# A decoder kernel's first loads: the first row and its norm parameters on ScalarE's queue

## The chip, the cores and the metric

The kernel runs on one core of a Trainium2 chip. The metric is the device time of one execution in microseconds. A core has five engines with a program each: TensorE (PE, with its weight loads as PEld), VectorE (DVE), ScalarE (ACT), GpSimd (POOL) and SyncE (SP). SP computes nothing; it issues transfers (DMAs). ScalarE and GpSimd can issue transfers too. An engine takes its instructions in order and waits at each until what it needs is there.

## The reference

Two layers on a residual x of 512 tokens by 1024: differential softmax attention, then retention, each followed by a squared-ReLU MLP and a gated embedding. Only the first step matters here: a norm, and the projection to queries, keys and values.

```
def rms_norm(x, g):
    y = x * rsqrt(mean(x * x, axis=-1) + EPS)
    return y * g
...
h = rms_norm(x, norm_mix[0])
qkv = h @ a_w_qkv          # values first in this kernel: 1024 x 1024
...
lam = exp(sum(lam_q1 * lam_k1)) - exp(sum(lam_q2 * lam_k2)) + lambda_init
```

## The kernel before

The residual lies transposed: eight rows of tiles xT[k], each 128 features by 512 tokens in float32 (256 KB). Precision is kept by splitting every factor into a high part (fp32r) and a low part, and multiplying three times: high by high (L188), high by low and low by high (L189, L190).

The weights come in tiles of 128x1024 (512 KB) by SP's queue into raw; ScalarE casts raw to wh (L84) and VectorE subtracts for wl (L88). There are three raw buffers and five of wh and wl. `W.load()` issues a tile; for the first tile W.parts is 2, and it comes in two halves of 256 KB.

The beginning works so. `sm` holds all small parameters, 128x311 floats: columns 0 to 15 are the gains of the mixers' norms (C_MIX), 16 to 31 those of the MLPs' norms (C_MLP on), then those of the embeddings' norms and the attention's gains, and at the end 256 columns of the lambda vectors. It is SP's first load. Then a loop over k = 0 to 7 loads row xin k of x, makes its scaled halves (`make_z`: zh = x times gain on ScalarE, L168; zl on VectorE, L169), loads a weight tile at each even k, and adds the squares of x (`squares`: ScalarE L234 for the first row and L237 for the others, GpSimd L238 adds them into acc_a). The norm's factor itself is applied behind the matmul, so that the projection doesn't wait for it.

TensorE first runs nine warm-up matmuls on a tile of ones (L288). Then the value projection goes over k, four accumulators (pv) a step: 12 matmuls for each k, two k to a weight tile, so raw0 serves k = 0 (first half) and k = 1 (second half), raw1 serves k = 2 and 3, raw2 k = 4 and 5.

The lambda factor (lp, ls, nlam) and the attention's gains (gq, gs) are written behind the projection in the source, at L341 to L355. The scheduler puts instructions of one engine in an order of its own, by when their inputs should be there; only loads marked keep_in_program_order stay in the order of the source.

Of the kernel before, what the change touches and what calls it, by code (L numbers as in the profile page):

```python
# [10 lines left out]
F32 = mybir.dt.float32  # L11
# [5 lines left out]
P = 128  # L17
# [3 lines left out]
KD = D // P  # L21
# [12 lines left out]
C_MIX, C_MLP, C_PE = 0, 16, 32  # L34
# [67 lines left out]
def decoder_trunk(ctx: ExitStack, tc, xT, pT, small, dist, decay, ident,  # L102
                  w_v, w_qk, w_o, w_up0, w1_0, w2_0, w_g0,
                  w_rv, w_rqk, w_rg, w_ro, w_up1, w1_1, w2_1, w_g1, out):
    nc = tc.nc

    gp = ctx.enter_context(tc.tile_pool(name="gp", bufs=1))
# [17 lines left out]
    def load(out, in_):  # L125
        tc.keep_in_program_order(nc.sync.dma_start(out=out, in_=in_))

    def slot(name, dt=F32):
        return gp.tile([P, T], dt, name=name, tag="slot", bufs=SLOTS)
# [96 lines left out]
    def make_z(src, gain_col, k, make=slot):  # L226
        zh = make(f"zh{gain_col}_{k}", F32R)
        zl = make(f"zl{gain_col}_{k}", F32R)
        split_into(zh, zl, src, sm[:, gain_col + k : gain_col + k + 1])
        return zh, zl  # L230

    def squares(acc, src, k, engine=None):
        if k == 0:
            tc.keep_in_program_order(nc.scalar.activation(out=acc, in_=src, func=AF.Square))  # L234
        else:
            sq = slot("sq")
            nc.scalar.activation(out=sq, in_=src, func=AF.Square)  # L237
            (engine or nc.gpsimd).tensor_tensor(out=acc, in0=acc, in1=sq, op=ALU.add)  # L238
# [33 lines left out]


    sm = gp.tile([P, N_SMALL], F32, name="sm")
    load(sm, small)
    eps = gp.tile([P, 1], F32, name="eps")
    nc.vector.memset(eps, EPS)
    ones = gp.tile([P, P], F32, name="ones")
    nc.vector.memset(ones, 1.0)
    ones_r = gp.tile([P, P], F32R, name="ones_r")  # L280
    nc.scalar.copy(out=ones_r, in_=ones)
    mhalf = gp.tile([P, 8], F32, name="mhalf")
# [8 lines left out]
    z = []  # L291
    W.parts = 2
    for k in range(KD):
        t = slot(f"xin{k}")
        load(t, xT[k])
        z.append(make_z(t, C_MIX, k))
        if k % 2 == 0:
            W.load()
            W.parts = 1
        squares(acc, t, k)  # L300
# [384 lines left out]
    with tc.tile_pool(name="zp", bufs=1) as zp:  # L685

        def zslot(name, dt):
            return zp.tile([P, T], dt, name=name, tag="z", bufs=16)
# [12 lines left out]
        with tc.tile_pool(name="ret", bufs=1) as ap:  # L701
# [36 lines left out]
            for h in range(RH):  # L738
# [22 lines left out]
                for n in range(4):  # L761
# [4 lines left out]
                    t = ap.tile([P, T], F32, name="rt", tag="rt", bufs=4)  # L766
# [21 lines left out]
                for jt in range(NT):  # L788
# [7 lines left out]
                    t = ap.tile([P, T], F32, name="rt", tag="rt", bufs=4)  # L796
# [40 lines left out]
            for m in range(KD):  # L837
                pu = (ps_tr if m % 2 == 0 else ps_s)(f"pu1{m}")
                up_unit(pu, wu, p1, m)
                t = zslot(f"pus{m}", F32)  # L840
# [90 lines left out]
```

## Time and profile before

| | us |
|---|---|
| median of 3 runs (1478.69 to 1480.45) | 1480.25 |
| the profiled execution | 1480.16 |
| its span, first to last instruction | 1478.0 |
| TensorE busy | 1468.3 (99%) |
| VectorE, ScalarE, GpSimd busy | 787.4, 650.6, 157.9 |
| chain that ended last: TensorE, ScalarE, VectorE | 94%, 3%, 2% |

The chain that ended last is followed back from the last instruction, at each step to what released it. A row of the timeline gives start, length, engine, line, operation, output and inputs, and in brackets the idle time before it with what ended it. Rows of loads give the size of one and the time from its issue to its landing.

### The profile page before, as it was taken

What the parts mean: (1) busy time and instruction counts of PE and PEld (TensorE: products, weight loads), DVE (VectorE), ACT (ScalarE), POOL (GpSimd) and SP (SyncE); (2) the same over time, 40 slices, a digit from 0 to 9 for tenths busy, and PEclk for the clock granted to TensorE, in tenths of its full rate; (3) what the DMA queues carried; (4) which work ended last, traced back from release to release, by engine and by line L of the source; (5) the groups of instructions that cost most, each with busy time, mean ns of one, the idle gap of its engine ahead of it and who ended that gap; (6) DMA issues with size and microseconds to landing.
All of it is one profiled execution on the core that took longest, in us unless ns stands there. A gap on an engine that the chain in (4) does not pass through costs nothing.

```text
span 1478.0 us, 17131 instructions
## 1 busy us (share of the span) xinstructions
PE 1468.3 (99%) x6668; PEld 1199.8 (81%) x6668; DVE 787.4 (53%) x1189; ACT 650.6 (44%) x1007; POOL 157.9 (11%) x127
## 2 busy tenths in 40 slices
PE   9999999999999999999999999999999999999998
PEld 7777677888888888888888888888878888888887
DVE  6775776643434434485464555553684343434445
ACT  6777777841423224354442532433553231323432
POOL 4112113100000000321120200301220000000020
PEclk9999999999999999999999999999999999999999
DMA  6654466853333332143223232132233233333212
GB/s 227 143 115 114 115 171 145 212 171 99 91 95 100 100 98 90 62 164 124 75 86 110 65 104 93 57 129 71 80 106 99 90 97 100 100 96 92 97 57 86
DMA packets 46880, 159.92 MB, mean 108 GB/s; under 512 B 5200, under 2 KB 5712, under 8 KB 46800
## 3 DMA queue, kind: packets, MB, share of 16 engines
q1 hardware_dynamic: 41328, 138.92, 29.3%
q0 software_dynamic: 4896, 17.83, 6.7%
q10 hardware_dynamic: 576, 2.10, 0.4%
q8 instruction: 52, 0.85, 0.2%
q14 instruction: 28, 0.23, 0.0%
HBM read 136.80 MB, written 4.19 MB: 95 GB/s over the span
## 4 chain that ended last, share of the span: by engine, by line
PE 94%; ACT 3%; DVE 2%; issue 1%; POOL 0%; DMA 0%; SPq 0%; POOLq 0%; ACTq 0%; DVEq 0%
PE py L190 8%; PE py L188 8%; PE py L189 8%; PE ph L188 8%; PE ph L190 8%; PE ph L189 8%; PE rg L188 2%; PE rg L189 2%; PE pg L188 2%; PE pg L189 2%; PE pg L190 2%; PE rv L188 2%; PE rv L190 2%; PE rqk L190 2%; PE rqk L188 2%; PE rv L189 2%
## 5 line engine op out<-in xcount | busy, mean ns | idle before, releaser
L84 ACT CAST wh<-raw 128x1024 fp32r<-128x1024 f32 (+1 forms) x211 | 221.0, 1049 | 603.0 <-PE py L189 235.7
L88 DVE TENSOR_TENSOR wl<-raw,wh 128x1024 fp32r<-128x1024 f32 (+1 forms) x211 | 267.2, 1267 | 54.6 <-ACT wh L84 53.3
L189 PE MATMUL ph<-zl,wh 128*128 128x512 f32 x512 | 199.4, 389 | 0.1
L188 PE MATMUL ph<-zh,wh 128*128 128x512 f32 x512 | 199.2, 389 | 0.0
L190 PE MATMUL ph<-zh,wl 128*128 128x512 f32 x512 | 199.2, 389 | 0.0
L188 PE MATMUL py<-hh,wh 128*128 128x512 f32 x512 | 199.2, 389 | 0.0
L189 PE MATMUL py<-hl,wh 128*128 128x512 f32 x512 | 199.2, 389 | 0.0
L190 PE MATMUL py<-hh,wl 128*128 128x512 f32 x512 | 199.2, 389 | 0.0
L628 DVE TENSOR_TENSOR x<-x,py 128x512 f32<-128x512 f32 x64 | 44.0, 688 | 200.0 <-PE py L190 200.0
L618 DVE SCALAR_TENSOR_TENSOR ht<-ph,rsm 128x512 f32<-128x512 f32 x64 | 44.1, 691 | 158.4 <-PE ph L190 158.2
L189 PEld LDWEIGHTS ph<-zl,wh 128*128 128x128 f32 x512 | 96.1, 188 | 20.9 <-DVE zl L169 0.9
L189 PEld LDWEIGHTS py<-hl,wh 128*128 128x128 f32 x512 | 96.1, 188 | 20.1
L190 PEld LDWEIGHTS py<-hh,wl 128*128 128x128 f32 x512 | 96.1, 188 | 20.0
L190 PEld LDWEIGHTS ph<-zh,wl 128*128 128x128 f32 x512 | 96.1, 188 | 20.0
L188 PEld LDWEIGHTS ph<-zh,wh 128*128 128x128 f32 x512 | 96.1, 188 | 19.9
L188 PEld LDWEIGHTS py<-hh,wh 128*128 128x128 f32 x512 | 96.1, 188 | 19.8
L238 POOL TENSOR_TENSOR acc_p<-acc_p,sq 128x512 f32<-128x512 f32 x14 | 24.5, 1751 | 649.2 <-ACT sq L237 649.2
L188 PE MATMUL pqk<-wh,zh 128*128 128x512 f32 x128 | 52.9, 413 | 0.0
L190 PE MATMUL pqk<-wh,zl 128*128 128x512 f32 x128 | 51.5, 402 | 0.0
L189 PE MATMUL pqk<-wl,zh 128*128 128x512 f32 x128 | 51.4, 401 | 0.0
L188 PE MATMUL pg<-zh,wh 128*128 128x512 f32 (+1 forms) x136 | 51.2, 377 | 0.0
L190 PE MATMUL pg<-zh,wl 128*128 128x512 f32 (+1 forms) x136 | 51.2, 377 | 0.0
(870 smaller groups left out, 2798.3 us busy)
## 6 DMA issues: line engine op xcount, KB each, us to landing
raw<-in_w SPq DMA_DIRECT2D x128, 512.0 KB, 3.6
wl<-raw POOLq DMA_DIRECT2D x34, 512.0 KB, 5.4
raw<-in_w_qk SPq DMA_DIRECT2D x16, 512.0 KB, 4.0
raw<-in_w_g SPq DMA_DIRECT2D x16, 512.0 KB, 3.5
raw<-in_w_rv SPq DMA_DIRECT2D x16, 512.0 KB, 3.6
raw<-in_w_rqk SPq DMA_DIRECT2D x16, 512.0 KB, 4.1
raw<-in_w_rg SPq DMA_DIRECT2D x16, 512.0 KB, 3.5
raw<-in_w_ro SPq DMA_DIRECT2D x16, 512.0 KB, 3.6
```

What stands on the lines that cost most here:

```text
L84: nc.scalar.copy(out=hi[:, s], in_=raw[:, s])
L88: e.tensor_tensor(out=lo[:, r], in0=raw[:, r], in1=hi[:, r].bitcast(F32), op=ALU.subtract)
L188: nc.tensor.matmul(ps, a[0], b[0], start=start, stop=False)
L189: nc.tensor.matmul(ps, a[0], b[1], start=False, stop=False)
L190: nc.tensor.matmul(ps, a[1], b[0], start=False, stop=stop)
L238: (engine or nc.gpsimd).tensor_tensor(out=acc, in0=acc, in1=sq, op=ALU.add)
L618: nc.vector.scalar_tensor_tensor(out=t, in0=s[1], scalar=0.0, in1=rs, op0=ALU.max, op1=ALU.mult)
L628: nc.vector.tensor_tensor(out=x[m], in0=x[m], in1=ps, op=ALU.add)
```

## The change

The load of sm is cut in two. Columns 0 to 15 (the mixers' gains, 64 bytes in a partition) and the first row xin0 are issued by ScalarE, as its first two instructions. The other 295 columns of sm are issued by SP behind xin1. SP's queue so begins with the two halves of the first weight tile. The tiles of all rows xin are claimed ahead of the loop, and the tile of ones is filled before eps.

```
-    load(sm, small)
+
+    def beside(out, in_):
+
+        tc.keep_in_program_order(nc.scalar.dma_start(out=out, in_=in_))
+
+
+    beside(sm[:, 0:C_MLP], small[:, 0:C_MLP])
+    xin = [slot(f"xin{k}") for k in range(KD)]
+    beside(xin[0], xT[0])
+    ones = gp.tile([P, P], F32, name="ones")
+    nc.vector.memset(ones, 1.0)
     eps = gp.tile([P, 1], F32, name="eps")
     nc.vector.memset(eps, EPS)
-    ones = gp.tile([P, P], F32, name="ones")
-    nc.vector.memset(ones, 1.0)
...
     for k in range(KD):
-        t = slot(f"xin{k}")
-        load(t, xT[k])
+        t = xin[k]
+        if k > 0:
+            load(t, xT[k])
+        if k == 1:
+            load(sm[:, C_MLP:], small[:, C_MLP:])
         z.append(make_z(t, C_MIX, k))
```

SP's queue at the start of the program, before. In all these rows the name's first number is the tile's (raw0, xin1), what follows an underscore is a buffer's number, and the brackets name the semaphores that an instruction waits on (DMAHW for a transfer, the others for an engine).

```order
L126 DMA sm_61<-in_small 128x311
L126 DMA xin0_82<-in_xT 128x512
L83 DMA raw0_88<-in_w_v 128x512 x2
L126 DMA xin1_98<-in_xT 128x512
L126 DMA xin2_107<-in_xT 128x512
L83 DMA raw1_113<-in_w_v 128x1024
```

SP's queue at the same place, now.

```order
L83 DMA raw0_95<-in_w_v 128x512 x2
L126 DMA xin1_64<-in_xT 128x512
L126 DMA sm_61<-in_small 128x295
L126 DMA xin2_65<-in_xT 128x512
L83 DMA raw1_119<-in_w_v 128x1024
```

raw0 comes first, and what is left of sm stands between xin1 and xin2.

ScalarE's queue from its first instruction to the cast of raw1, before.

```order
L281 ACT_TABLE_LOAD
L281 CAST ones_r_67<-ones_65 128x128 [waits DVE_49]
L346 ACTIVATE ls_324<-ls_324 128x2 [waits DVE_49]
L168 ACTIVATE zh0_0_84<-xin0_82,sm_61 128x512 [waits DMAHW1_49,DMAHW0_49]
L84 CAST wh0_89<-raw0_88 128x512 [waits DMAHW2_49]
L84 CAST wh0_89<-raw0_88 128x512 [waits DMAHW3_49]
L234 ACTIVATE acc_a_81<-xin0_82 128x512
L168 ACTIVATE zh0_1_100<-xin1_98,sm_61 128x512 [waits DMAHW4_49]
L237 ACTIVATE sq_104<-xin1_98 128x512
L168 ACTIVATE zh0_2_109<-xin2_107,sm_61 128x512 [waits DMAHW5_49]
L237 ACTIVATE sq_119<-xin2_107 128x512
L84 CAST wh1_114<-raw1_113 128x1024 [waits DMAHW6_49]
```

ScalarE's queue at the same place, now, up to zh of xin2.

```order
L278 DMA sm_61<-in_small 128x16
L278 DMA xin0_63<-in_xT 128x512
L289 ACT_TABLE_LOAD
L289 CAST ones_r_76<-ones_72 128x128 [waits DVE_49]
L84 CAST wh0_96<-raw0_95 128x512 [waits DMAHW1_49]
L168 ACTIVATE zh0_0_91<-xin0_63,sm_61 128x512 [waits DMAHW2_49,DMAHW0_49]
L84 CAST wh0_96<-raw0_95 128x512 [waits DMAHW3_49]
L234 ACTIVATE acc_a_90<-xin0_63 128x512
L168 ACTIVATE zh0_1_107<-xin1_64,sm_61 128x512 [waits DMAHW4_49]
L237 ACTIVATE sq_111<-xin1_64 128x512
L357 ACTIVATE ls_325<-ls_325 128x2 [waits DVE_49]
L168 ACTIVATE zh0_2_115<-xin2_65,sm_61 128x512 [waits DMAHW6_49]
```

Two issues stand ahead of the table load, and the exponential ls has moved from the front to a place between the squares of xin1 and zh of xin2.

VectorE's queue from the first use of sm to wl1, before.

```order
L343 TENSOR_TENSOR lp_322<-sm_61 128x128 [waits DMAHW0_49]
L352 TENSOR_SCALAR gq_330<-sm_61 128x1
L355 TENSOR_SCALAR gs_332<-sm_61 128x1
L345 TENSOR_REDUCE ls_324<-lp_322 128x2 [waits DVE_49]
L348 TENSOR_TENSOR nlam_327<-ls_324 128x1 [waits Activation_49]
L349 TENSOR_SCALAR nlam_327<-nlam_327 128x1 [waits DVE_49]
L169 SCALAR_TENSOR_TENSOR zl0_0_85<-xin0_82,sm_61,zh0_0_84 128x512 [waits DMAHW1_49,Activation_49]
L88 TENSOR_TENSOR wl0_90<-raw0_88,wh0_89 128x512 [waits DMAHW2_49,Activation_49]
L88 TENSOR_TENSOR wl0_90<-raw0_88,wh0_89 128x512 [waits DMAHW3_49,Activation_49]
L169 SCALAR_TENSOR_TENSOR zl0_1_101<-xin1_98,sm_61,zh0_1_100 128x512 [waits DMAHW4_49,Activation_49]
L169 SCALAR_TENSOR_TENSOR zl0_2_110<-xin2_107,sm_61,zh0_2_109 128x512 [waits DMAHW5_49,Activation_49]
L88 TENSOR_TENSOR wl1_115<-raw1_113,wh1_114 128x1024 [waits DMAHW6_49,Activation_49]
```

VectorE's queue at the same place, now.

```order
L88 TENSOR_TENSOR wl0_97<-raw0_95,wh0_96 128x512 [waits DMAHW1_49,Activation_49]
L169 SCALAR_TENSOR_TENSOR zl0_0_92<-xin0_63,sm_61,zh0_0_91 128x512 [waits DMAHW2_49,DMAHW0_49,Activation_49]
L88 TENSOR_TENSOR wl0_97<-raw0_95,wh0_96 128x512 [waits DMAHW3_49,Activation_49]
L354 TENSOR_TENSOR lp_323<-sm_61 128x128 [waits DMAHW5_49]
L363 TENSOR_SCALAR gq_331<-sm_61 128x1
L169 SCALAR_TENSOR_TENSOR zl0_1_108<-xin1_64,sm_61,zh0_1_107 128x512 [waits DMAHW4_49,Activation_49]
L356 TENSOR_REDUCE ls_325<-lp_323 128x2 [waits DVE_49]
L366 TENSOR_SCALAR gs_333<-sm_61 128x1
L359 TENSOR_TENSOR nlam_328<-ls_325 128x1 [waits Activation_49]
L360 TENSOR_SCALAR nlam_328<-nlam_328 128x1 [waits DVE_49]
L169 SCALAR_TENSOR_TENSOR zl0_2_116<-xin2_65,sm_61,zh0_2_115 128x512 [waits DMAHW6_49,Activation_49]
L88 TENSOR_TENSOR wl1_121<-raw1_119,wh1_120 128x1024 [waits DMAHW7_49,Activation_49]
```

The six instructions on the small parameters have moved from the front to places on both sides of zl of xin1. TensorE's order changes within the 12 matmuls of k = 0 only, and further on all engines' orders are as before.

## Rows read from the trace of the kernel before

**Rows 1.** The page's first lines: the span, and the chain's shares by engine.

```profile
span 1478.0 us, 17131 instructions
...
PE 94%; ACT 3%; DVE 2%; issue 1%; POOL 0%; DMA 0%; SPq 0%; POOLq 0%; ACTq 0%; DVEq 0%
```

**Rows 2.** The chain in order of time, first 12 us: start, length, what.

```profile
2.10 4.68 DMA raw<-in_w_v
...
6.80 0.62 ACT wh L84
...
11.20 2.10 DVE wl L88
```

**Rows 3.** Loads issued in the first 4 us: count, KB of one, us to landing.

```profile
sm<-in_small SPq DMA_DIRECT2D x1, 155.5 KB, 2.2
...
raw<-in_w_v SPq DMA_DIRECT2D x1, 256.0 KB, 3.3
...
raw<-in_w_v SPq DMA_DIRECT2D x1, 256.0 KB, 4.7
xin<-in_xT SPq DMA_DIRECT2D x1, 256.0 KB, 4.8
...
raw<-in_w_v SPq DMA_DIRECT2D x1, 512.0 KB, 6.0
```

**Rows 4.** Busy time by stretch: five engines, PEclk, DMA share, GB/s.

```profile
2.50:3.00 0.50, 0.50 (x5) 0.50 (x4) 0.03 (x1) 0.00 (x0) 0.00 (x0) 1.00 0.71 215
3.00:5.00 2.00, 2.00 (x11) 1.99 (x10) 1.15 (x7) 0.97 (x3) 0.00 (x0) 1.00 1.03 334
```

**Rows 5.** ScalarE's timeline, 0 to 12 us.

```profile
0.72 1.28 ACT L281 ACT_TABLE_LOAD   x1 [0.72 <-PEq L918]
...
3.62 0.20 ACT L346 ACTIVATE ls<-ls 128x2 f32<-128x2 f32 x1 [1.30 <-DVE ls L345]
...
8.48 0.62 ACT L237 ACTIVATE sq<-xin 128x512 f32<-128x512 f32 x1
...
10.13 1.04 ACT L84 CAST wh<-raw 128x1024 fp32r<-128x1024 f32 x1
```

**Rows 6.** VectorE's timeline, 2 to 14 us.

```profile
2.97 0.29 DVE L343 TENSOR_TENSOR lp<-sm 128x128 f32<-128x128 f32 x1 [1.93 <-DMA sm<-in_small]
...
7.46 0.69 DVE L88 TENSOR_TENSOR wl<-raw,wh 128x512 fp32r<-128x512 f32 x1 [1.16 <-ACT wh L84]
8.61 0.75 DVE L169 SCALAR_TENSOR_TENSOR zl<-xin,sm,zh 128x512 fp32r<-128x512 f32 x1 [0.46 <-ACT zh L168]
9.74 1.32 DVE L169 SCALAR_TENSOR_TENSOR zl<-xin,sm,zh 128x512 fp32r<-128x512 f32 x1 [0.38 <-ACT zh L168]
11.20 2.09 DVE L88 TENSOR_TENSOR wl<-raw,wh 128x1024 fp32r<-128x1024 f32 x1
```

**Rows 7.** GpSimd's second addition of squares.

```profile
10.59 1.62 POOL L238 TENSOR_TENSOR acc_a<-acc_a,sq 128x512 f32<-128x512 f32 x1
```

**Rows 8.** SP's issues, 0 to 4 us; ScalarE's issues of the whole kernel (ns).

```profile
0.73 0.38 SPq L126 DMA_DIRECT2D sm<-in_small  x1
...
1.63 0.90 SPq L83 DMA_DIRECT2D raw<-in_w_v  x2
2.57 0.91 SPq L126 DMA_DIRECT2D xin<-in_xT  x2
3.52 0.43 SPq L83 DMA_DIRECT2D raw<-in_w_v  x1
...
L563 ACTq DMA_DIRECT2D up<-pus x4: 326/326/348, 261.1 to 280.2; - x4
```

**Rows 9.** TensorE's timeline: first matmuls, and the wait for wl1.

```profile
5.62 1.59 PE L188 MATMUL pv<-wh,zh 128*128 128x512 f32 x4 [0.34 <-ACT wh L84]
...
11.60 1.07 PE L188 MATMUL pv<-wh,zh 128*128 128x512 f32 x4
13.35 0.50 PE L189 MATMUL pv<-wl,zh 128*128 128x512 f32 x1 [0.68 <-DVE wl L88]
```

## The prediction

> **What bounds the kernel now.** I began with the shares of the span and the chain that ended last. TensorE is busy for 99% of 1478.0 us and the chain is TensorE for 94% [rows 1]. So only time in which TensorE waits can be won, and the edit touches loads of the first microseconds alone: it can reach the waits before TensorE runs without a gap, and nothing behind them.
>
> The chain in order of time says where those waits end [rows 2]. It starts in the transfer of the second half of the first weights (raw0, landed at 2.10 + 4.68 = 6.78 us), goes through ScalarE from the second cast of raw0 (6.80) on, then through VectorE's subtraction wl1 (11.20 to 13.30), and enters TensorE at 13.35 [rows 9]. From there it is matmul behind matmul.
>
> The transfers come next [rows 3]. sm took 2.2 us from issue to landing, the first half of raw0 3.3, the second half 4.7. With the issues at 0.73, 1.63 and, in the second half of that row, 2.06 [rows 8] they landed at 2.9, 4.9 and 6.8. xin1, issued at 2.57, took 4.8 and landed at 7.4; raw1, issued at 3.52, took 6.0 and landed at 9.5. Two things are to be seen. The last half of raw0 came 1.85 us behind the first half, though the next 256 KB (xin1) came only 0.6 behind it: something held that transfer by about 1.2 us. And the transfer engines are the limit, not the issues: from 3 to 5 us they are busy for 103% and move 334 GB/s, with one dip from 2.5 to 3.0 (71%, 215 GB/s) [rows 4].
>
> ScalarE is busy without a gap from 6.80 until the cast of raw1 is done (10.13 + 1.04 = 11.17) [rows 5]; raw1 had long landed when it came to it. VectorE had gaps of 0.46 and 0.38 us there, but its wl1 took 2.09 [rows 6]. GpSimd adds squares at the same time: its second addition ended at 10.59 + 1.62 = 12.21 [rows 7], and wl1 ended 1.08 behind that, at 13.29. So wl1 was called when the cast was done, and held until GpSimd's addition was over; the chain view shows only the call.
>
> **The change, part by part.** Call T the start of the second cast of raw0 on ScalarE (6.80 before).
>
> *What T gains.* Before, 155.5 + 3 x 256 = 923.5 KB lie up to the end of raw0. Now it is 8 KB (128 rows of 16 floats) and the same 768 KB, on two queues; the other 147.5 KB of sm go behind xin1. At the measured 334 GB/s 151,000 bytes are 0.45 us. The first transfers are issued two at a time, so the dip should fill: 0.5 us at 215 in place of 334 GB/s is 0.18 us. Together 0.6 us. Bounds: no gain if the second queue only takes turns with the first and the small rows cost what is saved; at most 0.9 (raw0's halves are now SP's first two issues, so the second goes out some 0.9 us earlier) plus the 1.2 us of the hold, 2.1 us, if that doesn't come again. I take 0.6, since nothing in the rows says that the hold belonged to sm.
>
> *Small rows.* No row shows rows of 64 bytes. The nearest is sm itself, 128 rows of 1,244 bytes; 128 smaller ones cost between nothing and the 0.45 us of a whole sm. I take nothing, since they are issued ahead of the moment at which the engines are full.
>
> The Trainium skill (DMA: Bandwidth & Descriptors, section "Issuing engines are not separate DMA queues") says that transfers from any engine run on the same 16 transfer engines and that issuing from several saves only the sequencer's issue time. The full transfer engines of rows 4 agree with it; by it alone the gain at T would be the 0.45 us of bytes and no more.
>
> *ScalarE's two issues.* An issue costs SP 0.38 to 0.45 us, and ScalarE 0.33 in the only four that it has in this trace [rows 8]. Two of them push the table load of 1.28 us [rows 5] from 0.72 to about 1.5, the copy of ones to 3.1. The first weights can hardly land ahead of 3.3, so this is hidden; without that cover it would cost 0.7 to 0.85.
>
> *SP's queue.* It loses two issues and gets one. xin1 goes from 2.57 to about 1.63, ahead of sm's rest; xin2, raw1 and what follows have the same bytes ahead of them as before, so they gain the 0.18 us of the dip at most. raw1 at 9.3 is still ahead of its use.
>
> *The small parameters' arithmetic.* Six VectorE instructions (lp, gq, gs, the reduction, two for nlam) stood at 2.97 and behind it, and one exponential on ScalarE at 3.62, all in time in which these engines waited for transfers [rows 5, 6]. Now lp and gq stand between wl0 and zl1, the reduction behind zl1, and ScalarE's exponential between the squares of xin1 and zh2. That is an added wait: ScalarE comes to it at T + 2.3 (squares 8.48 + 0.62 = 9.10), but the reduction can only start when zl1 is over, 8.61 + 0.75 = 9.36 or T + 2.56 [rows 6], and, counted as lp, takes 0.29; the exponential takes 0.20. So zh2, which followed the squares directly, starts when the exponential is over, at T + 3.05 and not T + 2.3, and behind it wait the squares of xin2 and the cast of raw1, which is done at T + 5.1 instead of T + 4.4: 0.75 us late. Much of it falls into the time in which wl1 waited for GpSimd anyhow. GpSimd's second addition needs the squares of xin2, which were over when the cast of raw1 began (10.13, T + 3.3 to 3.4), and are now at T + 4.1 to 4.2; it starts at T + 4.25 to T + 4.45 (behind zl2) in place of T + 3.79, runs 1.15 us (it ended at 12.21, and zl2, which it had to let through, at 11.06 [rows 6, 7]), and ends at T + 5.4 to T + 5.6; wl1 ends 1.08 later, T + 6.5 to T + 6.7, against T + 6.49. The cost is 0 to 0.25 us, and 0.75 if the hold by GpSimd were none. I take 0.25.
>
> *Behind wl1* VectorE and GpSimd go in turns as before, and the order of all engines behind the first rows is as before, so wl2 and TensorE shift by what wl1 shifts. The ceiling is TensorE itself: it would have been ready for wl1 at 11.60 + 1.07 = 12.67 instead of 13.35 (the row gives 0.68 of idle time), and it could start some 0.3 us earlier, as it waited 0.34 for the first cast [rows 9]. That is about 1.0 us.
>
> *Sum.* 0.6 - 0.25 = 0.35 us off the profiled execution's 1480.16 us (its span is 1478.0, and 2.16 lie around it): 1479.8. The median of the three runs is 1480.25, which would give 1479.9; I take 1479.8.
>
> **The rivals.**
> - *The hold was sm's.* If the 1.2 us don't come again, T gains 1.8, wl1 about 1.5, and TensorE becomes the limit: 1.0 us, 1479.2. For it speaks that the hold is the only one of its size in rows 3; against, that nothing ties it to sm.
> - *The second queue gives nothing.* The engines are full from 3 us, xin0 takes turns with raw0, and the small rows eat the dip. T gains 0.3 to 0.45, less the 0.25: 0.05 to 0.2 us, 1480.0. Rows 4 speak for it from 3 us on and against it for the dip. It is also how the edit could fail to do what it says. The rule of the Trainium skill quoted above would make it this case.
> - *Slower: the exponential waits for sm's rest.* lp stands ahead of zl1 on VectorE and needs the part of sm that now comes behind xin1. It lands about 0.6 + 0.45 = 1.05 us behind raw0; VectorE is free for it at T + 1.35 (7.46 + 0.69) and zl1 starts at T + 1.81 (8.61) [rows 6]. If a hold as that of raw0 strikes here (1.2 us), lp comes at T + 2.25, zl1 some 0.8 late, then the exponential, zh2 and wl1: 0.25 + 0.8 - 0.6 = 0.45 us slower, 1480.6. It decides from a landing later than about T + 1.4.
> - *Something outside the rows* (a run-to-run matter of the long rest) moves the time by over 0.2%: 1477 or 1483.
>
> **How the numbers follow.** Forecast 1479.8: 0.50. Hold gone, 1479.2: 0.20. Second queue gives nothing, 1480.0: 0.12. Slower by the exponential, 1480.6: 0.10. Outside: 0.08. The cases lie between 1479.2 and 1480.6; the three runs before lie up to 1.6 us below their median and 0.2 above, so I widen by 1.3 below and 0.6 above: 1477.9 to 1481.2. About 0.2% (3 us) is what a measurement of this kernel can tell from no change. No case but the last passes it, and I split that evenly: 0.04 faster, 0.92 the same, 0.04 slower.
>
> **What would show it.** In the profile of the changed kernel: the second cast of raw0 starts at about 6.2 (5.0 if the hold is gone, 6.4 or later if the queue gives nothing); the exponential starts about 2.8 us behind it and ScalarE shows a wait of 0.5 on the reduction ahead of it; wl1 ends 6.5 to 6.7 behind T, near 12.9; TensorE's wait for wl1 shrinks from 0.68. The table load starts near 1.5 and nobody waits for it. The prediction is wrong if xin0 lands later than raw0, if the time moves by more than 1.5 us, or if TensorE's first gap-free matmul doesn't move with wl1.

## The result, and the profile after

The changed kernel took 1494.84 us (median of 4 runs, 1493.96 to 1496.03), the kernel before 1480.28 (4 runs, 1478.69 to 1480.45): 1.0103 of it, with a 95% interval of 1.0091 to 1.0114. It is slower by 14.6 us. The prediction was 1479.8 us and "the same" at 0.92, with a range up to 1481.2. It was wrong by about ten times the width that it allowed upward, and by its own measure (3 us can be told from no change) the kernel is slower and not "the same".

The profiled execution took 1495.05 us. The page's first lines, with the chain's shares, answer to [rows 1].

```profile
span 1493.3 us, 17131 instructions
...
PE 1483.0 (99%) x6668; PEld 1198.3 (80%) x6668; DVE 786.8 (53%) x1189; ACT 650.7 (44%) x1007; POOL 156.9 (11%) x127
...
PE 94%; DVE 2%; ACT 2%; issue 1%; POOL 0%; DMA 0%; ACTq 0%; POOLq 0%
```

The span grew by 15.3 us and TensorE's busy time by 14.7 (1468.3 before). So TensorE waits only 0.6 us more: with the same 6668 instructions it is busy for longer. A cause that works through a wait for another engine or a transfer can explain no more than these 0.6 us.

Where in the span it happens is read from one instruction that comes once in each layer. These are the pieces of the chain at line 267 (start, length, what), of before, then of after.

```profile
29.27 0.79 PE prst L267 x8
...
677.72 0.79 PE prst L267 x8
```

```profile
29.80 0.79 PE prst L267 x8
...
685.20 0.79 PE prst L267 x8
```

The edited beginning, up to the first of them, cost 0.53 us. From the first to the second it is 648.45 us before and 655.40 after, 6.95 more; and from there to the end 7.8 more (800.3 and 808.1). The loss lies all along the kernel, in stages that the edit doesn't name.

Which matmuls became slower is told by groups that keep shapes apart (line, engine, operation, output and inputs, shape, count; then busy time in us, mean ns of one, and idle time before them). Before:

```profile
L189 PE MATMUL ph<-zl,wh 128*128 128x512 f32 x512 | 199.4, 389 | 0.1
...
L188 PE MATMUL py<-hh,wh 128*128 128x512 f32 x512 | 199.2, 389 | 0.0
...
L189 PE MATMUL rx<-gol,wh 128*128 128x512 f32 x128 | 49.8, 389 | 0.0
...
L190 PE MATMUL pu<-p0h,wl 128*128 128x512 f32 x16 | 6.3, 395 | 0.0
...
L189 PE MATMUL pg<-zl,wh 128*128 128x256 f32 x16 | 4.5, 283 | 0.0
```

After:

```profile
L189 PE MATMUL ph<-zl,wh 128*128 128x512 f32 x512 | 201.9, 394 | 0.0
L190 PE MATMUL ph<-zh,wl 128*128 128x512 f32 x512 | 201.7, 394 | 0.0
L188 PE MATMUL ph<-zh,wh 128*128 128x512 f32 x512 | 201.7, 394 | 0.0
L189 PE MATMUL py<-hl,wh 128*128 128x512 f32 x512 | 199.3, 389 | 0.0
...
L189 PE MATMUL pg<-zl,wh 128*128 128x256 f32 x16 | 4.4, 276 | 0.0
```

The matmuls ph (z by the MLP's first weights) went from 389 to 394 ns, in all three products; py (h by its second weights), with the same shape, count and lines, stayed at 389. The mean of one includes the pipeline, in which matmuls overlap; what counts is the distance from start to start. Two rows of ph that are 14 matmuls apart, before, and two that are 13 apart, after, show it (start, length):

```profile
299.65 0.39 PE L188 MATMUL ph<-zh,wh 128*128 128x512 f32 x1
...
302.82 0.39 PE L190 MATMUL ph<-zh,wl 128*128 128x512 f32 x1
```

```profile
302.73 0.39 PE L188 MATMUL ph<-zh,wh 128*128 128x512 f32 x1
...
305.77 0.39 PE L189 MATMUL ph<-zl,wh 128*128 128x512 f32 x1
```

That is 226.4 and 233.8 ns; over all 1536 the traces give 227.2 and 233.4. The groups rx and pg became slower in the same way (both to 233.3 from 226.8 and 226.9), and the attention's output projection by less than half as much, 238.6 to 241.5. The groups rv, rqk and rg did not; pu, a small group, was at 394 to 396 already before. The 48 half-width matmuls of pg (128x256) went the other way, from 283 to 276 ns. In pqk the weights are the moving operand and the ring's tiles stand still; it lost 1 to 2 ns (413, 402 and 401 before, 415, 403 and 402 after). In numbers: 1536 ph, 384 rx, 360 pg and 192 of the output projection, about 2,470 matmuls; the 14.8 us behind the beginning are 6.0 ns for each, if all of them are put down to these groups.

What the slow groups share is where their moving operand lies. ph, rx and pg stream from a ring of 30 tiles (the tiles that `slot` hands out, xin the first of them), with wh or wl as weights. py streams from hh and hl, rv, rqk and rg from a pool of their own. The change claims the eight xin tiles ahead of ones, eps, ones_r and mhalf, and so the ring has slid down in memory by 1088 bytes, which is 64 modulo 256. These are the built programs' byte addresses within a partition:

```
                 ring (first tile)   wh        zh of the second pool   hh
before           18848               92576     133536                  172448
changed          17760               92576     133536                  172448
modulo 256       160 -> 96           160       160                     160
```

Every tile of these groups has a length that is a multiple of 256 bytes, so all tiles of a group have the same place modulo 256. Before, the ring lay at the place of wh and wl; now it lies 64 bytes off. That is the theory (A) which the runs below test, in two forms: A1, the ring's own address is a bad one; A2, what counts is the distance between moving tile and weights, modulo some power of two. The rival (B) is that it comes from the new order of loads.

### The profile page after: what moved, and what is told of

It is laid out like the page before. It is cut to its first block, busy times and chain, and to the rows that moved or that the text cites. A ratio compares the mean times of both kernels' runs of the same rounds, so it can differ in the third digit from the quotient of the medians.

```text
span 1493.3 us, 17131 instructions
## 1 busy us (share of the span) xinstructions
PE 1483.0 (99%) x6668; PEld 1198.3 (80%) x6668; DVE 786.8 (53%) x1189; ACT 650.7 (44%) x1007; POOL 156.9 (11%) x127
## 4 chain that ended last, share of the span: by engine, by line
PE 94%; DVE 2%; ACT 2%; issue 1%; POOL 0%; DMA 0%; ACTq 0%; POOLq 0%
PE ph L189 8%; PE ph L190 8%; PE ph L188 8%; PE py L189 8%; PE py L188 8%; PE py L190 8%; PE pg L190 2%; PE pg L189 2%; PE pg L188 2%; PE rg L188 2%; PE rg L189 2%; PE rqk L189 2%; PE rv L189 2%; PE rqk L188 2%; PE rv L188 2%; PE rv L190 2%
## 5 line engine op out<-in xcount | busy, mean ns | idle before, releaser
L189 PE MATMUL pg<-zl,wh 128*128 128x512 f32 (+1 forms) x136 | 51.8, 381 | 0.0
```

The lines of the kernel that those rows point to most:

```text
L189: nc.tensor.matmul(ps, a[0], b[1], start=False, stop=False)
```

## The experiments

**The changed kernel with the old addresses.** Only the claims of four tiles are moved ahead of the ring.

```
     sm = gp.tile([P, N_SMALL], F32, name="sm")
+    eps = gp.tile([P, 1], F32, name="eps")
+    ones = gp.tile([P, P], F32, name="ones")
+    ones_r = gp.tile([P, P], F32R, name="ones_r")
+    mhalf = gp.tile([P, 8], F32, name="mhalf")
...
```

> The changed kernel with one edit: eps, ones, ones_r and mhalf are claimed ahead of the first slot again, so the ring of 30 slots lies at the byte address of the kernel before (18848 in a partition) and not at 17760; the loads, their queues and the order of all engines are as in the changed kernel. Theory A (the address of the slots makes the matmuls that stream from them slower): the 14.7 us go away but for what the first 30 us lost, 0.5 us: 1480.8, and the groups of ph, pg and rx are back at 389 ns. Theory B (the two issues on ScalarE's queue, or the later first row, disturb the whole run): it stays at 1494 to 1495.

Measured: 1480.6 us (10 runs, 1478.98 to 1482.34), 1.0004 of before (0.9994 to 1.0013). The group ph:

```profile
L189 PE MATMUL ph<-zl,wh 128*128 128x512 f32 x512 | 199.4, 389 | 0.1
```

With all loads as changed, the loss is gone. So the order of loads isn't the cause.

**The kernel before with the new addresses.** All loads are on SP and in the old order; only the xin tiles are claimed behind sm.

```
     load(sm, small)
+    xin = [slot(f"xin{k}") for k in range(KD)]
...
-        t = slot(f"xin{k}")
+        t = xin[k]
```

> The kernel before with one edit: the tiles of the eight first rows are claimed right behind sm, so the ring of slots lies at 17760 as in the changed kernel; all loads are issued by SP in the old order, and the order of all engines is that of the kernel before. Theory A (addresses): slower by the 14.2 us that the changed kernel lost behind its first 30 us: 1494.4, with ph, pg and rx at 394 to 395 ns and py, rv, rqk at 389. Theory B (ScalarE's queue): 1480.3, no change.

Measured: 1494.83 us (4 runs, 1494.61 to 1495.35), 1.0102 of before (1.0087 to 1.0117). ph, and py beside it:

```profile
L189 PE MATMUL ph<-zl,wh 128*128 128x512 f32 x512 | 202.0, 395 | 0.0
...
L188 PE MATMUL py<-hh,wh 128*128 128x512 f32 x512 | 199.2, 389 | 0.0
```

The whole loss is here without any change of a load. Theory A holds, B is out.

**Offsets alone.** A kernel that leaves the decoder out: it loads one tile and runs 24 matmuls 128x512 for each of 38 pairs of offsets, with nothing else at work but three short additions on VectorE.

```
+    for m, s in combos:
+        ps = pp.tile([P, T], F32, name=f"m{4 * m}b_s{4 * s}b", tag="ps", bufs=4)
+        n = 24
+        for i in range(n):
+            o = s + 128 * (i % 4)
+            nc.tensor.matmul(ps, st[:, o : o + P], mv[:, m : m + T], start=i == 0, stop=i == n - 1)
```

> Not the decoder: it computes none of it and writes a filler. One tile of weights and one streamed tile, both starting at a multiple of 128 bytes, and groups of 24 matmuls of 128x512 (fp32r) that differ in the byte offset of the streamed tile (0 to 112 in steps of 16, then 128 to 4096) and of the weights (0, 32, 64, 96); nothing else runs. Theory A1 (the streamed operand's own place within 128 bytes decides): 226 to 227 ns a matmul at 32, 233 at 64 and 96, whatever the weights' offset; 0 unknown, between 213 and 233. Theory A2 (the place of one against the other decides, two reads of TensorE that meet): 226 to 227 wherever both offsets are equal, 233 where they differ by 32 or 64. If neither matters here, the other engines' traffic has a part in it.

It took 243.64 us. Its timeline (start, length of 24, output by its two offsets in bytes: m moving, s weights; the two tiles begin at the same place modulo 256):

```profile
22.74 5.60 PE L127 MATMUL m0b_s0b<-mv,st 128*128 128x512 f32 x24
28.18 5.72 PE L127 MATMUL m16b_s0b<-mv,st 128*128 128x512 f32 x24
33.74 5.77 PE L127 MATMUL m32b_s0b<-mv,st 128*128 128x512 f32 x24
...
44.93 5.67 PE L127 MATMUL m64b_s0b<-mv,st 128*128 128x512 f32 x24
...
111.46 5.76 PE L127 MATMUL m0b_s64b<-mv,st 128*128 128x512 f32 x24
...
189.44 5.64 PE L127 MATMUL m96b_s96b<-mv,st 128*128 128x512 f32 x24
...
200.47 5.73 PE L127 MATMUL m128b_s0b<-mv,st 128*128 128x512 f32 x24
206.04 5.61 PE L127 MATMUL m256b_s0b<-mv,st 128*128 128x512 f32 x24
211.49 5.60 PE L127 MATMUL m512b_s0b<-mv,st 128*128 128x512 f32 x24
```

A start subtracted from the next group's start, over 24, is the pace. Equal offsets: (28.18 - 22.74) / 24 = 226.7 ns. Moving tile 32 above: (39.34 - 33.74) / 24 = 233.3, with 39.34 the start of the next group. Weights 64 above, which is the case of the changed kernel: from 111.46 to the next group at 117.06, 233.3. 128 apart: 232.1. 256 and 512 apart: 227.1 and 226.7. Both at 96: from 189.44 to 194.91, 227.9, close to equal offsets at 0. So the distance counts, and it is back at nothing after 256 bytes. Already 16 bytes above make a difference (231.7), but 16 below make none (226.7 to 227.1 in three pairs), and 64 above cost less than the 233 that was expected: (50.44 - 44.93) / 24 = 229.6, with 50.44 the start of the next group. It needs no traffic of any other engine.

**All tiles moved together by 32 bytes.** The kernel before, with a small tile ahead of sm; ring, wh, wl and all behind them move alike.

```
+    pad = gp.tile([P, 8], F32, name="pad")
+    nc.vector.memset(pad, 0.0)
     sm = gp.tile([P, N_SMALL], F32, name="sm")
```

> The kernel before with a tile of 32 bytes claimed ahead of sm: every tile of the main pool and of the pools behind it lies 32 bytes further, so slots, weights and the MLP's hidden tiles all start at 64 within 128 bytes instead of 32, and keep their distances to each other. Theory A1 (own place): nearly all matmuls of 512 columns stream from 64 and are slow, some 5,000 x 6.8 ns = 34 us: about 1514. Theory A2 (one against the other): within 0.2% of 1480.3.

Measured: 1480.02 us (10 runs, 1479.19 to 1481.11), 1.0002 of before (0.9993 to 1.0011), ph and py at 389. A1 falls as far as one shift can show it.

**The changed kernel with 192 and with 64 bytes between ring and weights.** In both the ring stays at 17760; what lies behind mhalf, the weights among it, moves up.

```
     nc.vector.memset(mhalf, -0.5)
+    pad = gp.tile([P, 48], F32, name="pad")
+    nc.vector.memset(pad, 0.0)
```

The second run has 16 in place of 48 columns.

> The changed kernel, with one tile of 192 bytes more, claimed behind mhalf and so between the ring and the weight tiles. The ring stays at byte 17760; raw, wh, wl and all behind them move up by 192 (wh to 92768), so that ring and wh are again at the same place modulo 256 (96 and 96). Loads and order are those of the changed kernel. Theory A2 (what counts is the distance between the streamed tile and the weights, modulo 256): ph back to a mean of 389 and the whole to 1480.6 us as in the run with the old addresses, 1479.5 to 1481.8. Rival (the byte address of the ring itself counts, 17760 is a bad one): 1494.8 us, ph at 394.

> The changed kernel, with one tile of 64 bytes more behind mhalf, so that ring (17760, 96 modulo 256) and wh (92640, 224 modulo 256) lie 128 apart modulo 256. In the offsets alone a distance of 128 had 232.1 ns from start to start, 5.4 over equal places, against 6.4 for the 64 of the changed kernel. With a period of 256 bytes: 14.6 x 5.4 / 6.4 = 12.3 us over the kernel before, about 1492.5 us (1491.5 to 1494), ph at 393 to 394. With a period of 128 bytes (or of 64): 1480.6 us and ph at 389.

Measured: with 192 bytes 1479.81 us (11 runs, 1479.24 to 1480.69), 1.0000 of before (0.9991 to 1.0009). With 64 bytes 1494.36 (4 runs, 1494.09 to 1496.54), 1.0102 (1.0088 to 1.0116). ph of the first and of the second:

```profile
L189 PE MATMUL ph<-zl,wh 128*128 128x512 f32 x512 | 199.4, 390 | 0.1
```

```profile
L189 PE MATMUL ph<-zl,wh 128*128 128x512 f32 x512 | 202.3, 395 | 0.0
```

The first is the changed kernel, ring at the "bad" address, and 15 us faster for 192 unused bytes: A2 is shown. The second rules out a period of 128 or less. Its size was forecast too low, 12.3 us for 14.0, and the time lies just above the range that was given: 128 bytes apart cost here as much as 64, and in the offsets alone 1.2 ns less.

**The loads by themselves.** Two runs on what the edit was about, both with the old addresses. In the first, SP issues sm's first columns, xin0, raw0, xin1, sm's rest; in the second, ScalarE issues sm's first columns and SP the rest, from xin0 on.

```
-    beside(sm[:, 0:C_MLP], small[:, 0:C_MLP])
+    load(sm[:, 0:C_MLP], small[:, 0:C_MLP])
...
-    beside(xin[0], xT[0])
+    load(xin[0], xT[0])
```

The second run has only the second pair of lines.

> The order of the loads alone, without ScalarE's queue and without the move in memory: eps, ones, ones_r and mhalf are claimed ahead of the ring (byte 18848 as before), and SP issues sm's first 16 columns, xin0, raw0's halves, xin1, sm's other columns, xin2, raw1. Theory (the start alone is worth some tenths of a microsecond): xin0 lands near 3.6, the first cast has its half of raw0 near 4.6, the second cast starts at 6.3 to 6.4 (0.45 us of bytes less ahead of it), wl1 ends near 13.0, the time within 1.5 us of the kernel before (1479.0 to 1481.0). Rival (the second queue is what matters for the start): xin0 as late as 6.2 here too, or wl1 at 13.3 or later; the time would not tell the two apart, the rows do.

> As the run with all loads on SP, but sm's first 16 columns are issued by ScalarE, and SP begins with xin0, then raw0. Old addresses. If xin0 came late in the changed kernel (6.19 us) because it took turns with raw0, both being in flight from two queues: xin0 lands near 3.3 here, zh0 is at 3.6 to 4.0 or as soon as the first columns are there, the second cast at 6.2 to 6.4. If it came late because whatever ScalarE issues at the start is slow: zh0 waits for sm until 5 or later, although only 8 KB are on that queue. The time is within 1.5 us of the kernel before in either case (1479.0 to 1481.0).

Measured: 1479.75 us (11 runs, 1478.65 to 1480.7), 0.9999 of before (0.9990 to 1.0008); and 1478.9 us (11 runs, 1478.43 to 1479.62), 0.9993 (0.9984 to 1.0001). Loads issued in the first 1.4 us (KB of one, us to landing), of the changed kernel, of the first and of the second run:

```profile
raw<-in_w_v SPq DMA_DIRECT2D x2, 256.0 KB, 3.9
xin<-in_xT ACTq DMA_DIRECT2D x1, 256.0 KB, 5.0
sm<-in_small ACTq DMA_DIRECT2D x1, 8.0 KB, 3.0
```

```profile
xin<-in_xT SPq DMA_DIRECT2D x1, 256.0 KB, 2.6
sm<-in_small SPq DMA_DIRECT2D x1, 8.0 KB, 1.8
```

```profile
xin<-in_xT SPq DMA_DIRECT2D x1, 256.0 KB, 2.8
raw<-in_w_v SPq DMA_DIRECT2D x1, 256.0 KB, 3.0
sm<-in_small ACTq DMA_DIRECT2D x1, 8.0 KB, 2.9
```

xin0 took 5.0 us while it shared the transfer engines with raw0 (4.1 to 4.4 in the three other runs with these loads), and 2.6 to 2.8 where it stood ahead of raw0 in one queue. That fits a delay by the sharing. But the 8 KB of sm took 2.9 to 3.0 us from ScalarE and 1.8 from SP, so ScalarE's queue may have a part in it; xin0 from ScalarE with nothing beside it wasn't run. In the changed kernel zh0 waits for xin0; in the second run it waits for sm's first columns, as this row of its ScalarE shows, but only until 3.69.

```profile
3.69 0.72 ACT L168 ACTIVATE zh<-xin,sm 128x512 fp32r<-128x512 f32 x1 [0.93 <-DMA sm<-in_small]
...
6.24 0.62 ACT L84 CAST wh<-raw 128x512 fp32r<-128x512 f32 x1 [1.32 <-DMA raw<-in_w_v]
```

The second cast still waits, until 6.24: raw0's second half came 4.6 us after its issue here. The first run has less of this: its second cast came at 6.06, after a wait of 0.26 and earlier than the 6.3 to 6.4 expected, and its first at 5.18 where 4.6 was expected. wl1 ended at 12.86 in the first (13.0 expected) and at 13.05 in the second. The second run is the fastest of all, 1.4 us below the kernel before and 0.1 below the range that was given for it; the interval still touches 1, so a gain is possible and not shown.

## Why the prediction was wrong, step by step

**The step that failed** is the third sentence of the prediction: the edit "can reach the waits before TensorE runs without a gap, and nothing behind them", with its twin, that "the order of all engines behind the first rows is as before, so wl2 and TensorE shift by what wl1 shifts". The order is indeed as before, and TensorE does run without a gap. But a kernel whose chain is TensorE for 94% [rows 1] is priced by the pace of its matmuls, and the edit could change that pace: it changes in which order tiles are claimed, and so where 30 tiles lie. The front part says so in a clause (the tiles "are claimed ahead of the loop"), and the prediction never costed it; it looked at order and transfers alone. Beside the tiles' addresses one row of before held the hint, and even the size: pu, which streams from tiles 64 bytes below the weights' place in the first layer (as the ring does now) and 32 above in the other, stood at 395 beside ph's 389, with the same shape. These 6 ns for 2,470 matmuls are 14.8 us. The case for causes "outside the rows" had 0.08, with prices of 1477 and 1483; its mechanism was said to be a run-to-run matter, which it isn't: the loss comes and goes with the addresses in every run above.

**T, the second cast of raw0.** Forecast 6.2, measured 6.91. ScalarE's timeline of the changed kernel, which answers to [rows 5]:

```profile
1.65 1.28 ACT L289 ACT_TABLE_LOAD   x1 [1.65 <-PEq L929]
...
3.62 0.62 ACT L84 CAST wh<-raw 128x512 fp32r<-128x512 f32 x1 [0.38 <-DMA raw<-in_w_v]
6.28 0.72 ACT L168 ACTIVATE zh<-xin,sm 128x512 fp32r<-128x512 f32 x1 [2.04 <-DMA xin<-in_xT]
6.91 0.60 ACT L84 CAST wh<-raw 128x512 fp32r<-128x512 f32 x1
...
9.68 0.20 ACT L357 ACTIVATE ls<-ls 128x2 f32<-128x2 f32 x1 [0.49 <-DVE ls L356]
```

The prediction sized T by the bytes ahead of raw0. What ended the wait was xin0, which landed at 1.17 + 5.02 = 6.19, behind raw0: zh0 stands ahead of the second cast on ScalarE, and the cast then starts without a wait. That xin0 might take turns with raw0 was in the second rival, but priced by raw0's landing and not by the instruction that stands in front of the cast; and "xin0 lands later than raw0" was named as a sign that the prediction is wrong. Three other runs have the same loads, and in them too zh0 waited for xin0 behind raw0: T was 6.03 (old addresses), 5.96 and 6.26 (192 and 64 bytes). Against the 6.80 of before, 0.6 us looks like a fair size for these three. But the two other runs with the loads of before had 6.65 (new addresses) and 6.15 (all shifted by 32 bytes), so the two sets overlap, and the 0.6 us are neither shown nor refuted. One profile of these first microseconds is no measurement of them.

**The dip** did fill, though this was worth nothing here: from 2.5 to 3.0 us 336 GB/s in place of 215 [rows 4].

```profile
2.50:3.00 0.50, 0.50 (x4) 0.50 (x4) 0.00 (x0) 0.49 (x2) 0.00 (x0) 1.00 1.05 336
```

**ScalarE's two issues** took 0.41 and 0.45 us (forecast up to 0.45), the table load began at 1.65 (forecast 1.5), and nobody waited for it. **Small rows** were taken at nothing; the 8 KB landed 3.0 us after their issue, ahead of xin0, and cost nothing.

**The exponential** was right within a few hundredths: 9.68 is T + 2.77 (2.8 was forecast), with 0.49 of waiting for the reduction (0.5). **wl1** ended at 13.73, T + 6.82, where 6.5 to 6.7 stood. VectorE's, GpSimd's and TensorE's rows, for [rows 6, 7, 9]:

```profile
11.99 1.74 DVE L88 TENSOR_TENSOR wl<-raw,wh 128x1024 fp32r<-128x1024 f32 x1 [0.50 <-ACT wh L84]
```

```profile
11.16 1.49 POOL L238 TENSOR_TENSOR acc_a<-acc_a,sq 128x512 f32<-128x512 f32 x1 [0.55 <-ACT sq L237]
```

```profile
7.05 0.50 PE L188 MATMUL pv<-wh,zh 128*128 128x512 f32 x1 [1.81 <-ACT zh L168]
...
12.67 1.07 PE L188 MATMUL pv<-wh,zh 128*128 128x512 f32 x4
13.79 0.51 PE L189 MATMUL pv<-wl,zh 128*128 128x512 f32 x1
```

wl1 now waits 0.50 for the cast and runs in 1.74 rather than 2.09. It again ends 1.08 behind GpSimd's second addition (11.16 + 1.49 = 12.65), and that addition started at T + 4.25 as forecast; the term that was mis-sized is its length, 1.49 and not 1.15. So wl1 came 0.33 us later behind T than before, where 0.25 was taken. TensorE's wait of 0.68 for wl1 is gone as forecast, but not because wl1 is early: TensorE itself starts late (7.05 for 5.62), for zh0, and from there runs without a gap. The stall went from wl1 to xin0. The four kernels with these loads reached the first row of line 267 at 29.80, 28.80, 30.19 and 29.28 us, and the three with the loads of before at 29.27, 29.22 and 29.08. So no gain at the beginning is shown, where 0.35 us were forecast. Nor do the whole times show one where the distance is nothing: the changed loads gave 1.0004 and 1.0000 of before, with intervals of about 0.1% (1.4 us) to either side.

**The rivals.** "The hold was sm's" is not borne out: raw0's second half is as late (4.6 us) in the run where only 8 KB of sm are ahead of it, though the rest of sm was then issued 1 us behind it; and the second cast started at 6.15 in the kernel before shifted by 32 bytes, where all of sm stands in front. What holds the transfer stays open. "The second queue gives nothing" named turns between xin0 and raw0, which fit the rows, but in the wrong place. "The exponential waits for sm's rest" didn't happen: VectorE took lp without a wait. None of these three was priced at more than 1 us, and nearly all of the 14.6 came from what none of them spoke of.

## What to carry to other kernels

An edit that claims tiles in another order moves all tiles of that pool, and in this kernel, where TensorE is busy for 99%, a move of 64 bytes cost more than any change of the loads: print the tiles' addresses of both versions and compare them, modulo 256, for each pair of moving tile and weights. When TensorE's busy time grows at an unchanged number of instructions, compare the mean of each group of matmuls with the same shape; here a group that differed from its twin by 5 ns was the place. What is worth less than a microsecond at the beginning can't be read from one profile of it: the same loads gave a spread of 1.4 us.

## What the hardware showed that was not expected

**Moving tile against weights.** In the offsets alone a matmul of 128x512 in fp32r follows the one before it after 226.7 to 228.3 ns when the two operands' addresses are equal modulo 256, and after 230.8 to 235.0 ns in most other cases (moving tile 64 above: 229.2 to 229.6, 16 below: 226.7 to 227.1). In this kernel 2,470 such matmuls are 14.6 us, 1.0%. It is no rule for every shape: the 128x256 matmuls of pg started 119.8 ns apart with equal places and 113.4 with the moving tile 64 below; why is open, and no other type was run. The Trainium skill (SBUF — State Buffer, section "Who interferes with whom") gives TensorE two read ports, one for the moving operand and one for loading weights, and calls them independent. The rows of the offsets alone, in which next to nothing but TensorE works, show that the pace does depend on where the two operands lie to each other; whether they meet at these ports or elsewhere is not shown by any run here.

**A slow pace at the start.** In the run with all loads on SP TensorE waited for 0.60 us between warm-up and first step, and then ran its matmuls about 0.43 us apart for 3.6 us. Two of its rows, and its stretch from 8 to 9 us (busy time of five engines, then granted clock, DMA share, GB/s):

```profile
8.15 0.63 PE L190 MATMUL pv<-wh,zl 128*128 128x512 f32 x1
8.57 0.63 PE L189 MATMUL pv<-wl,zh 128*128 128x512 f32 x1
```

```profile
8.00:9.00 1.00, 1.00 (x3) 0.72 (x3) 0.86 (x3) 0.51 (x3) 0.58 (x1) 1.00 0.98 379
```

The granted clock reads 1.00, the level of 2.4 GHz, and yet the pace is about half of the 0.23 us of the changed kernel, which had waited for 1.81 us and ran at full pace from its second matmul on. The run with 192 bytes had a like stretch of 4.0 us after a wait of 0.86, the one with old addresses had none after 0.93. From TensorE's first matmul of the projection to the four ahead of wl1 it took 7.60 us with 192 bytes (6.11 to 13.71) and 5.58 with old addresses (6.18 to 11.76), and the first row of line 267 came 1.4 us later; these two runs are the ends of the spread at the beginning. The cause is open.
